# ConvFFN of a two-layer backbone: issue order of tiles 2 to 20 written out on four engines, partial sums grown in PSUM, all low parts of up weights on VectorE

## The chip, the cores and the metric

The kernel runs on one core of one Trainium2 chip. The metric is the device time of one execution in microseconds (us), the median of several runs. A profile is one execution taken by the hardware profiler. In it PE is the matrix engine (TensorE) and PEld its weight loads, DVE is VectorE, ACT is ScalarE, POOL is GpSimd, and SP is the queue that issues most DMAs. L306 means line 306 of the kernel's file.

## The reference

Two trunk layers run over 1024 latent tokens and (in the first layer only) 256 context tokens, all in float32, with 1024 channels. A layer is a mixer followed by a ConvFFN. This case is about the ConvFFN, which is the larger part of the time:

```python
def conv_ffn(h, w_up, conv_w, conv_b, w_down):
    L = h.shape[1]
    a = h @ w_up
    gate, val = a[..., :D_FF], a[..., D_FF:]
    gp = jnp.pad(gate, ((0, 0), (CONV_W // 2, CONV_W // 2), (0, 0)))
    g = gp[:, 0:L] * conv_w[0] + gp[:, 1:1 + L] * conv_w[1] + gp[:, 2:2 + L] * conv_w[2] + conv_b
    return (jax.nn.silu(g) * val) @ w_down
...
        x = x + g2 * conv_ffn(modulate(x, norm2_g[layer], sh2, sc2), ...)
```

D_FF is 2816. In the first layer (layer 0) latent and context tokens both pass through it, in the second (layer 1) only the latent tokens.

## The kernel before

**Precision.** Every float32 operand of a matmul is split into a high and a low part (`split`, L445 to L448): ACT writes the high part as a rounded copy (L447), then DVE or POOL writes the low part as source minus high part (L448). A product is three matmuls per chunk of 128 rows: high by high, high by low, low by high (`PASSES`).

**Halves and tiles.** The tokens of a layer are worked off in two halves: the positions of a half lie in two blocks of n columns (n is 320 and 324 in layer 0, 256 and 258 in layer 1). D_FF is cut into 22 tiles (f = 0 to 21) of 128 channels. So there are four halves of 22 tiles each, in order of time: two of layer 0, two of layer 1.

**The up projection of a tile** (`up`, L274) uses a seven-product scheme for a 2 by 2 block matrix product instead of eight. The weights of a tile form four blocks, A00 and A01 (gate), A10 and A11 (value); from these come the sums S1 = A10 + A11 (L241), S3 = A00 - A10 (L247), S2 = S1 - A00 (L248) and S4 = A01 - S2 (L251), all on POOL. Seven of these are weights of a product: A00 (P1), A01 (P2), S2 (P6), S1 (P5), S3 (P7), A11 (P4), S4 (P3). A product is 12 matmuls (4 chunks by 3 passes, L306), so a tile has 84. The moving operands (tile `hs`) are split once for each half in `operands`. The results are added to four blocks: c00 and c01 are the gate at the first and the last n positions, c10 and c11 the value. Every product has a PSUM bank of its own (tag `pq`, 8 banks in rotation); ACT copies P1 to c00 (L323), and seven DVE additions (L311) build the rest:

```python
add(c10, x["P6"], c00); add(c00, c00, x["P2"]); add(c01, x["P5"], c10)
add(c10, c10, x["P7"]); add(c11, c10, x["P5"]); add(c10, c10, x["P4"]); add(c01, c01, x["P3"])
```

**The gate.** ACT writes g = C0 * w1 + bias (L315, tile `g`, one buffer); DVE adds the two outer taps of the width-3 convolution (L317, L319; two pieces each in layer 0, where latent and context columns lie side by side, one each in layer 1); ACT applies Silu in place (L321); DVE multiplies with the value C1 (L361); the result is split into `act` (L362, so L447 on ACT and L448 on DVE).

**The down projection** (`down`, L368) runs beside it: in tile f it works on pairs of finished tiles, four output blocks D0 to D3 per tile (`downs`). Each is 12 matmuls of n columns (L376; in the first half of layer 1 it is 6 of 512 columns), and DVE adds it to the residual stream times a gain (L382). I call these additions X0 to X3. `prep` splits the down weights of a later tile (tile `wd`, two splits per tile) and issues the DMA of the next raw down weights (`fetch`, L261).

**Weights ahead.** During tile f the weights of tile f+1 are split, block by block, into slots that its products will read (tiles `wh` and `wq`, `steps`), and the raw blocks of tile f+2 are loaded: `load0` (A00, A01) and `load1` (A10, A11), 512 KB each (L236, tile `wr`, two buffers, so a load waits until the blocks that lie there are used up). When `load1` has landed, POOL makes S1 into the one buffer of tile `ws` (L241). While down projections run (`busy`), the low parts of A00, A01 and A11 are made by POOL (`POOL`, L245), those of the other four by DVE.

**Order.** The program is written tile by tile; a scheduler with its own model of time then sets the order on each engine, with `high_priority` for the additions, the gate and the `act` split. Engines run their instructions in the order so set, one after the other. Tiles 0 and 1 of a half hold no down projection; `beside` (`BESIDE`) adds small steps to tiles 1 to 3: in the first half of a layer the normalised input of the second half (L152, L153, with DMAs to a scratch in DRAM), in the second half of layer 0 sums of squares (L642, L644) and one square root (L658) for the next layer. Tile 21 holds no down projection either; the rest of them follows it.

## Time and profile before

| | us |
|---|---|
| median of 3 runs | 2914.65 (2911.54 to 2923.23) |
| the profiled execution's own time | 2920.99 |
| its span, first to last instruction | 2919.1 |

The mean granted clock of the profiled execution is 0.974 of full speed. Its time lies 6.3 us above the median of the runs, and 1.9 us of it lie outside the span. By the 88 groups of 84 up-projection matmuls the four halves stand at 486.8 to 926, 953.9 to 1378, 2107.9 to 2486 and 2512.3 to 2889 us of the span (from the first matmul of tile 0 to the end of tile 21's products); the mixers lie before and between the layers. "Stretch" below is a piece of the span; busy times in it are those of each engine, the number in brackets counts instructions.

### The profile page before, as it was taken

How to read it: one execution, taken by the hardware profiler on the slowest of the kernel's cores; microseconds unless marked ns; L12 is line 12 of the kernel's file. 1: busy time of each engine (PE TensorE's matmuls, PEld its weight loads, DVE VectorE, ACT ScalarE, POOL GpSimd, SP SyncE). 2: the span in 40 equal slices, each digit the busy share in tenths (PEclk: the TensorE clock that was granted, in tenths of full speed). 3: DMA queues.
4: the chain of work that ended last, by engine and by line, in shares of the span. 5: the costliest groups of instructions: out<-in, count | busy, mean ns of one | idle time of the engine just before them, and what ended most of it. 6: DMA issues, size and time to landing. Idle time of an engine off the chain costs nothing.

```text
span 2919.1 us, 47590 instructions
## 1 busy us (share of the span) xinstructions
PE 2772.8 (95%) x17978; PEld 2522.4 (86%) x17978; DVE 2216.9 (76%) x3748; ACT 1302.0 (45%) x2448; POOL 1267.9 (43%) x1044
## 2 busy tenths in 40 slices
...
GB/s 303 215 189 118 98 217 72 112 74 86 80 87 101 75 80 87 73 81 87 24 169 101 137 109 183 180 179 80 37 109 101 95 87 98 105 89 93 94 88 95
DMA packets 335886, 327.67 MB, mean 112 GB/s; under 512 B 16217, under 2 KB 264617, under 8 KB 335657
## 3 DMA queue, kind: packets, MB, share of 16 engines
...
q14 instruction: 86, 0.70, 0.1%
...
## 4 chain that ended last, share of the span: by engine, by line
PE 61%; DVE 14%; DMA 7%; POOL 7%; issue 5%; ACT 5%; SPq 0%; POOLq 0%; DVEq 0%; ACTq 0%
PE pq L306 18%; PE pq L478 15%; PE pq L376 11%; PE ps L478 6%; DMA wr<-in_ffn_w_up_dram 4%; POOL ws L241 2%; DVE xl L382 2%; DVE wh L448 2%; PE pq L566 2%; POOL wh L448 2%; DVE hx L311 2%; PE ps L487 2%; ACT t L1227 1%; POOL wr L248 1%; DMA wd<-in_ada_w_dram 1%
## 5 line engine op out<-in xcount | busy, mean ns | idle before, releaser
L376 PE MATMUL pq<-act,wd 128*128 128x320 f32 (+3 forms) x3696 | 639.8, 322 | 59.3 <-DVE xl L382 24.5
L376 PEld LDWEIGHTS pq<-act,wd 128*128 128x128 f32 x3696 | 557.1, 193 | 92.0 <-DVE xl L382 28.7
L306 PE MATMUL pq<-hs,wh 128*128 128x320 f32 (+3 forms) x4128 | 607.5, 299 | 16.3 <-DVE xl L382 7.8
L306 PEld LDWEIGHTS pq<-hs,wh 128*128 128x128 f32 x4128 | 576.9, 191 | 26.4 <-DVE xl L382 11.2
L306 PE MATMUL pq<-hs,wq 128*128 128x320 f32 (+3 forms) x3144 | 469.8, 299 | 8.4 <-DVE wq L448 4.9
L478 PE MATMUL pq<-hs,wh 128*128 128x512 f32 (+3 forms) x2100 | 469.0, 358 | 3.6 <-DVE hs L724 1.9
L306 PEld LDWEIGHTS pq<-hs,wq 128*128 128x128 f32 x3144 | 442.5, 191 | 14.1 <-DVE wq L448 5.7
L478 PEld LDWEIGHTS pq<-hs,wh 128*128 128x128 f32 x2100 | 365.8, 193 | 78.0 <-issue 6.2
L241 POOL TENSOR_TENSOR ws<-wr 128x512 f32<-128x512 f32 x88 | 153.6, 1745 | 397.3 <-DMA wr<-in_ffn_w_up_dram 333.0
L447 ACT ACTIVATE wh<-wr 128x512 fp32r<-128x512 f32 (+1 forms) x223 | 161.8, 726 | 354.0 <-POOL wr L248 201.5
L382 DVE SCALAR_TENSOR_TENSOR xl<-pq,mod,xl 128x320 f32<-128x320 f32 (+5 forms) x616 | 304.1, 514 | 11.7 <-PE pq L376 11.6
L448 DVE TENSOR_TENSOR wh<-wr,wh 128x512 fp32r<-128x512 f32 (+1 forms) x147 | 166.9, 1135 | 184.8 <-ACT wh L447 184.5
L448 POOL TENSOR_TENSOR wq<-wr,wq 128x512 fp32r<-128x512 f32 x152 | 235.7, 1550 | 32.9 <-ACT wq L447 32.9
L478 PE MATMUL ps<-hs,wh 128*128 128x512 f32 x840 | 240.0, 405 | 3.6 <-ACT hs L721 1.8
L311 DVE TENSOR_TENSOR hx<-hx,pq 128x320 f32<-128x320 f32 (+3 forms) x440 | 196.1, 448 | 29.1 <-PE pq L306 21.6
L447 ACT ACTIVATE wq<-wr 128x512 fp32r<-128x512 f32 x262 | 160.0, 623 | 101.3 <-PE pq L306 73.2
L447 ACT ACTIVATE wh<-ws 128x512 fp32r<-128x512 f32 x172 | 107.5, 625 | 169.8 <-PE pq L306 115.4
L478 PEld LDWEIGHTS ps<-hs,wh 128*128 128x128 f32 x840 | 141.9, 191 | 41.6 <-issue 14.4
L251 POOL TENSOR_TENSOR ws<-wr 128x512 f32<-128x512 f32 x88 | 120.2, 1366 | 123.3 <-DVE wh L448 112.3
L999 POOL TENSOR_TENSOR hsp<-hsq,hsp 128x512 fp32r<-128x512 f32 (+1 forms) x40 | 47.1, 1185 | 265.5 <-ACT hsq L998 265.5
L1006 DVE RECIPROCAL hsq<-hsq 128x512 f32<-128x512 f32 (+1 forms) x40 | 121.1, 3030 | 52.9 <-ACT hsq L1005 52.1
L448 DVE TENSOR_TENSOR wd<-wrd,wd 128x512 fp32r<-128x512 f32 x176 | 155.5, 912 | 0.2 <-ACT wd L447 0.2
...
## 6 DMA issues: line engine op xcount, KB each, us to landing
...
adaw<-in_ada_w_dram SPq DMA_DIRECT2D x128, 256.0 KB, 3.6
...
```

The lines of the kernel that those rows point to most:

```text
L241: op(raw["S1"], raw["A10"], raw["A11"], ALU.add)
L251: op(x, raw["A01"], raw["S2"], ALU.subtract)
L306: nc.tensor.matmul(o, w[wn][:, wp, k], self.part(s, bn, k, sp), start=(k == 0 and i == 0), stop=(k == 3 and i == 2))
L311: nc.vector.tensor_tensor(o, x, y, ALU.add)
L376: nc.tensor.matmul(pd, self.wds[j][i][:, wp, d % 4], self.acts[f][:, sp, lo:lo + m], start=(i == 0 and pi == 0), stop=(i == len(fs) - 1 an ...
L382: nc.vector.scalar_tensor_tensor(x, pd[:, a - lo:b - lo], net.mod[:, self.layer, st, 5, d:d + 1], x, ALU.mult, ALU.add)
L447: self.nc.scalar.activation(h, src, AF.Copy)
L448: return (e or self.nc.vector).tensor_tensor(l, src, f32(h), ALU.subtract)
L478: nc.tensor.matmul(o, w(wp, k), s(k, sp), start=(ki == 0 and pi == 0), stop=(ki == len(order) - 1 and pi == 2))
L487: nc.tensor.matmul(out, l[a], r[b], start=(first and i == 0), stop=(last and i == 2))
L566: nc.tensor.matmul(acc[32 * q:32 * q + 32, 0:256], self.sT[:, k, :], w[q // 2][:, 256 * (q % 2):256 * (q % 2) + 256], start=(k == 0), stop ...
L1006: nc.vector.reciprocal(r, r)
```

## The change

Four things change, all in `Ffn`, and all in tiles 2 to 20 of each half (those with `downs`).

1. **Order.** `run` opens a region at f = 2 and closes it at f = 21, in which PE, DVE, ACT and POOL issue in the order in which the program is written; SP's order is still the scheduler's. Inside it a tile is written as a list of tokens, `STEADY` (`STEADY2` for tile 2). A product is P1 to P7; D0 to D3 are the down blocks; X0 to X3 their additions to the residual; w with a name is a step of the weights (split, load or sum); c00, U, V and c10 are copies by ACT; c00+, c11+ and c01+ are additions by DVE; a token with a minus at its end belongs to the tile before. So Silu, the multiplication, the `act` split and X2 and X3 of a tile now stand among the first instructions of the next.
2. **Sums in PSUM.** P6 is accumulated onto P1's bank, P7 onto the same, and P4 onto the same (not in tile 2); P3 onto P5's bank. Between them ACT copies the bank out: P1 to c00, P1 + P6 to c01 (U), P1 + P6 + P7 to c10 (V), and with P4 to c10 again. DVE is left with c00 + P2, c11 = c10 + P5 and c01 + (P5 + P3). Matmuls are as many as before.
3. **Low parts.** `POOL` is empty: the low parts of A00, A01 and A11 are made by DVE. POOL keeps the four sums.
4. **Tile 1** leaves its Silu, multiplication and `act` split to tile 2.

```diff
-    POOL = ("A00", "A01", "A11")
+    POOL = ()
+    STEADY = ("P1", "silu-", "X2-", "X3-", "P2", "c00", "mul-", "wA00", "P6", "acth-", "c00+", "actl-", "wA01", "P5",
...
-        def product(p):
+        def product(p, onto=None):
             wn, bn = self.PROD[p]
-            o = net.t(net.ps, [P, 512], "pq" if p in ("P2", "P5") else "pq")[:, :n]
+            o = net.t(net.ps, [P, 512], "pq")[:, :n] if onto is None else onto
...
+                    nc.tensor.matmul(o, w[wn][:, wp, k], self.part(s, bn, k, sp),
+                                     start=(onto is None and k == 0 and i == 0), stop=(k == 3 and i == 2),
+                                     skip_group_check=onto is not None)
...
+            onto = dict(P6="P1", P7="P6", P3="P5")
+            if f > 2:
+                onto["P4"] = "P7"
+            ops = {"c00": lambda: copy(c00, x["P1"]), "c00+": lambda: add(c00, c00, x["P2"]),
+                   "U": lambda: copy(c01, x["P6"]), "V": lambda: copy(c10, x["P7"]),
+                   "c11+": lambda: add(c11, c10, x["P5"]), "c10": lambda: copy(c10, x["P4"]),
+                   "c10+": lambda: add(c10, c10, x["P4"]), "c01+": lambda: add(c01, c01, x["P3"]),
+                   "gate": gate, "taps": taps, "prep": prep}
...
+                if f == 2:
+                    region = self.net.tc.manual_schedule(engines={engines.PE, engines.DVE, engines.Activation, engines.Pool})
+                    region.__enter__()
+                if f == NF - 1:
+                    region.__exit__(None, None, None)
```

In `STEADY` the tile goes on: P5, U, P7, prep, D0, V, wS1, c11+, P4, wS2, X0, D1, c10, wS3, wload0, P3, wA11, wload1, X1, D2, c01+, gate, wS4, taps, D3, ws. On PE that is P1 P2 P6 P5 P7 D0 P4 D1 P3 D2 D3.

Three pieces show what this does to the order. The first is POOL in the second half of layer 1, one tile from its S1 on; before, it reads:

```order
L241 TENSOR_TENSOR ws_26590<-wr_26536 128x512
L247 TENSOR_TENSOR wr_26536<-wr_26500,wr_26536 128x512
L448 TENSOR_TENSOR wh_20746<-wr_26500,wh_20746 128x512
L448 TENSOR_TENSOR wq_20648<-wr_26500,wq_20648 128x512
L248 TENSOR_TENSOR wr_26500<-ws_26590,wr_26500 128x512
L251 TENSOR_TENSOR ws_26590<-wr_26500 128x512
L448 TENSOR_TENSOR wq_20973<-wr_26536,wq_20973 128x512
```

With the change the same engine there, up to the S1 of the next tile (lines are the changed file's):

```order
L248 TENSOR_TENSOR ws_26280<-wr_26242 128x512
L254 TENSOR_TENSOR wr_26242<-wr_26226,wr_26242 128x512
L255 TENSOR_TENSOR wr_26226<-ws_26280,wr_26226 128x512
L258 TENSOR_TENSOR ws_26280<-wr_26226 128x512
L248 TENSOR_TENSOR ws_26479<-wr_26441 128x512
```

The three low parts (`wh` and `wq`) are gone, and S2 (the third row now) no longer stands behind two of them.

The second piece is DVE at the turn of a tile in the same half: the last addition to c01, S4's low part (`wh` from `ws`), the taps (`g`), residual additions (`xl`), down weights (`wd`) and the multiplication (`g` from `hx`). Before:

```order
L311 TENSOR_TENSOR hx_26596<-hx_26596,pq_26742 128x258
L448 TENSOR_TENSOR wh_20747<-ws_26590,wh_20747 128x512
L382 SCALAR_TENSOR_TENSOR xl_3782<-pq_26760,mod_127,xl_3782 128x256
L382 SCALAR_TENSOR_TENSOR xl_3782<-pq_26768,mod_127,xl_3782 128x258
L317 SCALAR_TENSOR_TENSOR g_26597<-hx_26596,cols_175_786,g_26597 128x515
L382 SCALAR_TENSOR_TENSOR xl_3793<-pq_26776,mod_127,xl_3793 128x256
L382 SCALAR_TENSOR_TENSOR xl_3793<-pq_26784,mod_127,xl_3793 128x258
L319 SCALAR_TENSOR_TENSOR g_26597<-hx_26596,cols_175_786,g_26597 128x515
L448 TENSOR_TENSOR wd_26846<-wrd_26648,wd_26846 128x512
L448 TENSOR_TENSOR wd_26849<-wrd_26648,wd_26849 128x512
L361 TENSOR_TENSOR g_26597<-g_26597,hx_26596 128x516
```

With the change:

```order
L323 TENSOR_TENSOR hx_26282<-hx_26282,pq_26339 128x258
L524 TENSOR_TENSOR wh_20565<-ws_26280,wh_20565 128x512
L335 SCALAR_TENSOR_TENSOR g_26283<-hx_26282,cols_175_786,g_26283 128x515
L337 SCALAR_TENSOR_TENSOR g_26283<-hx_26282,cols_175_786,g_26283 128x515
L447 SCALAR_TENSOR_TENSOR xl_3782<-pq_26445,mod_127,xl_3782 128x256
L447 SCALAR_TENSOR_TENSOR xl_3782<-pq_26452,mod_127,xl_3782 128x258
L447 SCALAR_TENSOR_TENSOR xl_3793<-pq_26465,mod_127,xl_3793 128x256
L447 SCALAR_TENSOR_TENSOR xl_3793<-pq_26472,mod_127,xl_3793 128x258
L348 TENSOR_TENSOR g_26283<-g_26283,hx_26282 128x516
L524 TENSOR_TENSOR wh_20564<-wr_26425,wh_20564 128x512
L323 TENSOR_TENSOR hx_26481<-hx_26481,pq_26501 128x258
L346 TENSOR_TENSOR act_26532<-g_26283,act_26532 128x516
```

Both taps now stand ahead of X2 and X3, the down weights have moved to the middle of the next tile, and A00's low part (`wh` from `wr`) has come from POOL.

The third piece is DVE later in that tile of the changed program, from the low part of A01 on (two of the rows with `wq`, those of A01 and A11, were POOL's before, as the first piece shows; `wd` are the down weights, `wh` from `ws` S1, `wh` from `wr` S2, the second `wq` S3):

```order
L524 TENSOR_TENSOR wq_20466<-wr_26425,wq_20466 128x512
L524 TENSOR_TENSOR wd_26564<-wrd_26371,wd_26564 128x512
L524 TENSOR_TENSOR wd_26567<-wrd_26371,wd_26567 128x512
L524 TENSOR_TENSOR wh_20565<-ws_26479,wh_20565 128x512
L323 TENSOR_TENSOR hx_26481<-hx_26481,pq_26538 128x258
L524 TENSOR_TENSOR wh_20564<-wr_26425,wh_20564 128x512
L447 SCALAR_TENSOR_TENSOR xl_2932<-pq_26572,mod_127,xl_2932 128x256
L447 SCALAR_TENSOR_TENSOR xl_2932<-pq_26579,mod_127,xl_2932 128x258
L524 TENSOR_TENSOR wq_20467<-wr_26441,wq_20467 128x512
L524 TENSOR_TENSOR wq_20791<-wr_26441,wq_20791 128x512
```

A tile now has nine low parts on DVE, seven of up weights and two of down weights, where it had six, and three additions where it had seven. Outside the ConvFFN tiles PE, DVE, ACT and SP issue the same operations in the same sequence as before.

More of the change, by code (lines that the diff above doesn't have):

```diff
@@ L320, in gate, with high, low @@
                                                ALU.mult, ALU.add)
-            nc.scalar.activation(g, g, AF.Silu)
-        x = {}
-        todo = [("P1", lambda: nc.scalar.activation(c00, x["P1"], AF.Copy)),
+        def high():
+            self.acts[f] = self.act()
+            nc.scalar.activation(self.acts[f][:, 0, :2 * h.n], g, AF.Copy)
+        def low():
+            a = self.acts[f]
+            self.tail = nc.vector.tensor_tensor(a[:, 1, :2 * h.n], g, f32(a[:, 0, :2 * h.n]), ALU.subtract)
+        after = {"silu": lambda: nc.scalar.activation(g, g, AF.Silu),
+                 "mul": lambda: nc.vector.tensor_tensor(g, g, C1, ALU.mult), "acth": high, "actl": low}
+        x = {}
+        before, self.before = self.before, {}
+        if steady:
+            onto = dict(P6="P1", P7="P6", P3="P5")
[6 more added lines that the diff above has]
+                   "gate": gate, "taps": taps, "prep": prep}
+            i = 0
+            for tok in self.STEADY if f > 2 else self.STEADY2:
+                if tok in self.PROD:
+                    x[tok] = product(tok, x[onto[tok]] if tok in onto else None)
+                    if i in beside:
+                        beside[i]()
+                    i += 1
+                elif tok[0] == "D":
+                    adds["X" + tok[1]] = downs[int(tok[1])]()
+                elif tok[-1] == "-":
+                    if tok[:-1] in before:
+                        before[tok[:-1]]()
+                elif tok[0] == "X":
+                    adds.pop(tok)()
+                elif tok[0] == "w":
+                    if tok[1:] in steps:
+                        steps[tok[1:]]()
+                else:
+                    ops[tok]()
+            self.before = dict(after, **adds)
+            return
+        for fn in before.values():
+            fn()
+        todo = [("P1", lambda: copy(c00, x["P1"])),
                 ("P1 P6", lambda: add(c10, x["P6"], c00)),
@@ L358, in up @@
                     steps[st]()
-        act = self.acts[f] = self.act()
+        if f == 1:
+            self.before = after
+            return
         with net.tc.high_priority():
-            nc.vector.tensor_tensor(g, g, C1, ALU.mult)
-            self.tail = net.split(act[:, 0, :2 * h.n], act[:, 1, :2 * h.n], g)
+            for fn in after.values():
+                fn()
     def blocks(self, s):
```

51 lines of the change are left out of this document (32 added, 19 removed).

## The prediction

> **What bounds the kernel now.** I read the page first, then the busy times by stretch, the waits of the last half, its chain of waits, and at last the costs of single operations. The page's first part says that PE is the engine to look at:
>
> ```profile
> PE 2772.8 (95%) x17978; PEld 2522.4 (86%) x17978; DVE 2216.9 (76%) x3748; ACT 1302.0 (45%) x2448; POOL 1267.9 (43%) x1044
> ```
>
> 95% is a mean over stages, so I cut the span at the tiles. The columns are the stretch, its length, busy time and instructions of PE, PEld, DVE, ACT and POOL, granted clock, DMA share and GB/s. The first four rows are one tile of each half in which PE never waits, the next four tiles 5 to 20 of each half, the next four tiles 2 to 4, the last two single late tiles.
>
> ```profile
> core 0: us, PE busy (x) PEld busy (x) DVE busy (x) ACT busy (x) POOL busy (x), PEclk, DMA share, GB/s
> 700.66:720.08 19.42, 19.42 (x135) 19.42 (x133) 18.32 (x33) 7.99 (x14) 10.14 (x7) 1.00 0.28 82
> 1030.55:1050.09 19.54, 19.54 (x134) 19.54 (x133) 16.59 (x35) 9.05 (x15) 10.89 (x7) 1.00 0.27 81
> 2257.64:2273.15 15.51, 15.51 (x110) 14.46 (x108) 10.80 (x18) 7.30 (x13) 9.14 (x7) 1.00 0.31 93
> 2630.41:2646.30 15.89, 15.89 (x134) 15.89 (x133) 11.25 (x23) 6.66 (x12) 11.72 (x7) 1.00 0.23 66
> 601.70:914.10 312.40, 310.86 (x2115) 310.42 (x2114) 286.27 (x497) 128.24 (x209) 174.72 (x113) 1.00 0.27 82
> 1050.10:1366.10 316.00, 315.62 (x2114) 313.09 (x2113) 289.10 (x498) 128.87 (x209) 172.21 (x112) 1.00 0.27 81
> 2204.70:2476.00 271.30, 256.01 (x1729) 235.57 (x1728) 207.80 (x335) 116.36 (x208) 162.31 (x112) 0.98 0.32 94
> 2594.40:2878.80 284.40, 263.44 (x2114) 260.96 (x2113) 214.93 (x402) 117.88 (x210) 182.20 (x112) 0.98 0.30 89
> 530.80:601.70 70.90, 62.88 (x398) 59.70 (x396) 69.30 (x114) 32.51 (x57) 36.34 (x24) 0.98 0.37 108
> 981.40:1050.10 68.70, 63.47 (x414) 62.09 (x413) 63.46 (x104) 34.30 (x57) 44.61 (x30) 0.98 0.26 77
> 2145.20:2204.70 59.50, 51.59 (x327) 47.06 (x326) 55.27 (x77) 30.88 (x51) 38.98 (x25) 0.91 0.31 99
> 2539.50:2594.40 54.90, 49.34 (x397) 47.97 (x397) 50.21 (x84) 24.52 (x43) 36.62 (x24) 1.00 0.28 81
> ...
> 2646.30:2664.40 18.10, 16.15 (x135) 15.95 (x134) 13.29 (x27) 7.27 (x13) 11.25 (x7) 1.00 0.31 95
> 2681.60:2701.30 19.70, 17.65 (x134) 17.44 (x133) 14.90 (x30) 8.34 (x15) 11.51 (x7) 0.92 0.35 104
> ```
>
> A tile that PE alone sets takes 19.42, 19.54, 15.51 and 15.89 us in the four halves. Sixteen of these are 310.7, 312.6, 248.2 and 254.2 us, so tiles 5 to 20 stand above PE's own time by 1.7, 3.4, 23.1 and 30.2 us. Layer 0 is at its bound, with DVE busy for 92% (286.27 of 312.40); layer 1 is not. Three tiles of PE's time are 58.3, 58.6, 46.5 and 47.7, so tiles 2 to 4 stand above it by 12.6, 10.1, 13.0 and 7.2. In all some 101 us can be had, no more, since the matmuls stay as they are.
>
> Why layer 1 waits is in the waits of its second half (engine, tile and line, what it waited for: total us, times, longest):
>
> ```profile
> ACT wh L447 <- POOL wr L248: 77.6, 15, 5.3
> POOL ws L241 <- DMA wr<-in_ffn_w_up_dram: 77.3, 14, 5.9
> PE pq L376 <- DVE xl L382: 21.0, 12, 2.3
> ```
>
> and in the chain of waits there (start, length, what):
>
> ```profile
> 2662.74 5.15 DMA wr<-in_ffn_w_up_dram
> ...
> 2668.03 3.09 POOL ws L241
> ...
> 2672.79 1.74 POOL wh L448
> ...
> 2675.74 1.29 POOL wr L248
> 2677.05 0.64 ACT wh L447
> ...
> 2698.22 4.79 DMA wr<-in_ffn_w_up_dram
> ```
>
> It is a ring: a load lands, POOL makes S1, S3, two low parts, then S2; ACT, in order, copies S2 at 2677.05; DVE, in order, makes its low part, then the residual additions, whose PSUM banks PE waits for (21.0 us); and the low parts that end this free the buffer for the next load. Two rounds take 2698.22 - 2662.74 = 35.5 us, 17.7 each, which is the mean tile (284.40 / 16 = 17.8), not PE's 15.89.
>
> **The change part by part.** Prices from the last half, then from tiles 8 to 19 of the first half (mean ns of one behind the busy time):
>
> ```profile
> L247 POOL TENSOR_TENSOR wr<-wr,wr 128x512 f32<-128x512 f32 x16 | 26.1, 1631 | 1.2
> L447 ACT ACTIVATE wh<-ws 128x512 fp32r<-128x512 f32 x32 | 20.0, 625 | 12.0 <-POOL ws L241 6.2 <-PE pq L306 5.8
> L315 ACT ACTIVATE g<-hx,cols,cols 128x516 f32<-128x516 f32 x17 | 13.9, 820 | 52.1 <-DVE hx L311 52.1
> L317 DVE SCALAR_TENSOR_TENSOR g<-hx,cols,g 128x515 f32<-128x515 f32 x17 | 12.7, 747 | 0.0
> L321 ACT ACTIVATE g<-g 128x516 f32<-128x516 f32 x16 | 10.2, 637 | 11.4 <-DVE g L319 11.4
> ```
>
> ```profile
> L319 DVE SCALAR_TENSOR_TENSOR g<-hx,cols,g 128x511 f32<-128x511 f32 x13 | 17.9, 1374 | 0.0
> L448 DVE TENSOR_TENSOR wd<-wrd,wd 128x512 fp32r<-128x512 f32 x24 | 15.3, 678 | 0.0
> L448 DVE TENSOR_TENSOR wh<-wr,wh 128x512 fp32r<-128x512 f32 x12 | 14.9, 1244 | 0.2 <-ACT wh L447 0.2
> L315 ACT ACTIVATE g<-hx,cols,cols 128x640 f32<-128x640 f32 x13 | 12.0, 923 | 4.0 <-DVE hx L311 3.4 <-ACT wh L447 0.3
> L311 DVE TENSOR_TENSOR hx<-pq,hx 128x320 f32<-128x320 f32 x24 | 11.5, 481 | 0.0
> L317 DVE SCALAR_TENSOR_TENSOR g<-hx,cols,g 128x511 f32<-128x511 f32 x13 | 9.7, 746 | 0.1
> L319 DVE SCALAR_TENSOR_TENSOR g<-hx,cols,g 128x127 f32<-128x127 f32 x12 | 9.3, 771 | 0.0
> L321 ACT ACTIVATE g<-g 128x640 f32<-128x640 f32 x12 | 8.9, 740 | 24.5 <-DVE g L319 24.5
> L317 DVE SCALAR_TENSOR_TENSOR g<-hx,cols,g 128x127 f32<-128x127 f32 x13 | 7.6, 588 | 0.0
> L323 ACT ACTIVATE hx<-pq 128x320 f32<-128x320 f32 x12 | 5.0, 417 | 0.0
> ```
>
> One thing stands out: the same low part takes 0.68 us on DVE (`wd`) or 1.24 (`wh` from `wr`), the same tap 0.75 or 1.37. The first of each pair runs while POOL rests or nearly so, the second while it works; the additions that read PSUM are short throughout. I call these the cheap and the dear price.
>
> *The ring of layer 1.* With the low parts gone from POOL, S2 is ready 5.15 + 3.09 + 1.63 + 1.29 = 11.2 us after the load is issued. Then follow ACT's copy (0.63), the low parts of S2, S3 and A11, which free the buffer, and X0 among them (two pieces, at most c01's 0.48 each, 1.0). At the cheap price that is 11.2 + 0.6 + 3 x 0.68 + 1.0 = 14.8 us, at the dear one 16.5. I take the cheap price, because POOL's only operation near these three is now S4's sum; 14.8 is below PE's 15.51 and 15.89, so PE sets the tile. With 0.1 us left over per tile, 16 x 15.6 = 249.6 and 16 x 16.0 = 256.0: the gain is 21.7 and 28.4 us.
>
> In that the clock has a share: the tiles of 18.10 and 19.70 us differ little in their wait but in the granted clock, 1.00 and 0.92, and where PE doesn't wait it is 1.00. The Trainium skill, "TensorE: Matmul & The Clock Gate" (What's actually happening), has the clock halve after an idle window of about 3.4 us. By that no wait of 2.3 us would cost clock and this stretch would gain its idle time alone, 284.40 - 263.44 = 21.0 instead of 28.4 us; the trace disagrees, and I go by the trace.
>
> *DVE's load.* Four additions go (4 x 0.48 = 1.9 us a tile) and three low parts come (2.0 cheap, 3.7 dear). In layer 0 DVE works 286.27 / 16 = 17.9 us a tile; that becomes 18.0 to 19.7, against 19.42. I take the cheap end, since POOL has four operations a tile instead of seven; the cover is thin, and the dear end would cost 0.3 x 38 = 11 us in layer 0. In layer 1, 13.4 becomes 13.5 to 15.2, below PE. ACT gets three copies of 0.42 on 8 us a tile, hidden.
>
> *The new wait.* P6 now adds to P1's bank, so PE must wait until ACT has copied P1, and ACT's order puts Silu of the tile before ahead of that copy. From the end of P3 the path is c01+, gate, the copy and the low part of S4 (which DVE does ahead of the taps), taps, Silu, copy. Queued behind it on PE are P5, P7 and all else, and on ACT U and V. In layer 0: 0.48 + 0.92 + 0.63 + 0.68 + (2 x 0.75 + 0.59 + 0.77) + 0.74 + 0.42 = 6.7 us, and six handovers between engines, for which I put 0.3 us (POOL's to ACT in the chain above took 0.02 us, from 2675.74 + 1.29 to 2677.05; the DMA's to POOL 0.14): 7.0. PE has D2, D3, P1 and P2 to do meanwhile, 48 of a tile's 132 matmuls: 19.42 x 48 / 132 = 7.06. In layer 1: 0.48 + 0.82 + 0.63 + 0.68 + 2 x 0.75 + 0.64 + 0.42 + 0.3 = 5.5 against 15.89 x 48 / 132 = 5.78. So it is hidden, barely. S1's sum on POOL can reach the taps only if the load lands early; it is issued near the end of P3 and takes 5 us, so I take the cheap price. At the dear one for S4's low part and the taps of full width, P6 would wait 8.8 - 7.06 = 1.7 us in layer 0 and 7.3 - 5.78 = 1.5 in layer 1.
>
> *Tiles 5 to 20 of layer 0.* Nothing much to gain: at 19.45 and 19.6 a tile, 1.2 and 2.4 us.
>
> *Tiles 2 to 4.* In the first half DVE is busy for 69.30 of 70.90 us. The steps of `beside` stay; each writes one buffer that a DMA must have read, and DVE now waits for it in order, and ACT's copy of P1 behind it. Between none of the excess and all of it removed I take half to six tenths in the first half and in those of layer 1 (8, 6.5 and 4.4 us). In layer 0's second half the square root comes, in ACT's order, ahead of the copy of P1 in tile 3, with two small additions before it: some five operations of 0.4 to 0.6 us, 3 us, so I take 2.7 of 10.1. Sum 21.6, bounds 43 (all) and -10 (each of the ten wide steps in tile 2 makes PE wait 1 us).
>
> *Sum.* 21.7 + 28.4 + 1.2 + 2.4 + 21.6 = 75.3 us. The profiled execution's own time of 2920.99 becomes 2845.7; it stands 6.3 us above the median, so 2914.65 - 75.3 = 2839.4, say 2840.
>
> **The rivals.**
>
> A, *P6 waits for the copy of P1* (slower). If POOL's S1 falls into the taps, tiles 2 to 20 of each half pay 1.7 us in layer 0 and 1.5 in layer 1: 38 x 1.7 + 38 x 1.5 = 122 us, 2840 + 122 = 2962. It decides from about 75 / 76 = 1.0 us a tile on. For it: 7.0 of 7.06 us; the dear taps of layer 0 are in the trace. Against it: S1 has to wait for a landing of about 5 us and for S4's low part, which stands ahead of the taps. The Trainium skill, "SBUF — State Buffer" (Who interferes with whom), makes this an exclusive lock: a DVE instruction with two SBUF inputs and a POOL instruction that reads SBUF exclude each other for a whole instruction, PSUM readers aside. The pairs 0.68 and 1.24, 0.75 and 1.37 agree.
>
> B, *the ring still sets layer 1*, at the dear 16.5 us: 32 x 16.5 = 528 of 271.3 + 284.4, a gain of 27.7 instead of 50.1. That gives 2862. For it: S1 took 3.09 us on POOL because DVE was at work, and DVE does more now. So the change would not do what it says there.
>
> **How the numbers follow.** Forecast 0.70, B 0.14, A 0.16, and of A 0.08 at its full price, 0.06 near two thirds of it (about 2921, no change), 0.02 below. About 0.5%, 14.6 us, is what a measurement of this kernel can tell: faster 0.86, same 0.06, slower 0.08. The low end of the range is all excess removed, 2914.65 - 101 = 2814; the high end takes in B, starts that gain nothing and the dear DVE load: 2862 + 21.6 + 11 = 2895. What is left out is A.
>
> **What would show it.** Right: tiles 5 to 20 at about 311, 314, 250 and 256 us by stretch, clock 1.00 there; four POOL operations a tile; no wait of ACT for S2's sum. Wrong: a wait of PE for ACT's copy of P1 in every tile (A); tiles of 16.5 us in layer 1 with PE waiting at P7 or at D2 (B); DVE busy for the whole of a layer 0 tile (its dear load); tiles 2 to 4 longer than now.

## The result and the profile after

The changed kernel takes 2966.09 us (2959.72 to 2970.28, 4 runs); the kernel before, on the same chip, 2914.90 (2911.54 to 2923.23, 4 runs). The ratio is 1.0169, with a 95% interval of 1.0141 to 1.0198. The change makes it slower by 1.7%, where 2840 us and a gain were forecast. The profiled execution takes 2966.70 us.

The page's first part for the changed kernel:

```profile
PE 2769.4 (93%) x17978; PEld 2515.7 (85%) x17978; DVE 2301.2 (78%) x3676; ACT 1354.3 (46%) x2672; POOL 872.7 (29%) x816
```

PE is busy for 2769 us as it was for 2773 before: the matmuls cost the same, and what came on top is waiting. POOL has lost a third of its work. Where the waiting lies is in the busy times by stretch (columns as in the prediction; first tiles 2 to 4 of the four halves, then tiles 5 to 20):

```profile
532.50:614.40 81.90, 63.98 (x398) 63.08 (x397) 66.06 (x111) 34.94 (x66) 21.28 (x16) 0.87 0.31 94
1009.67:1091.60 81.93, 66.95 (x414) 66.05 (x413) 65.02 (x99) 36.69 (x64) 30.64 (x21) 0.88 0.24 71
2195.24:2264.77 69.53, 51.42 (x326) 46.82 (x325) 58.74 (x80) 33.41 (x62) 23.09 (x16) 0.88 0.32 102
2594.32:2656.22 61.90, 50.26 (x398) 49.19 (x397) 56.62 (x84) 29.12 (x56) 23.21 (x16) 0.92 0.31 91
614.40:943.12 328.72, 314.19 (x2115) 310.02 (x2114) 294.45 (x484) 137.94 (x257) 92.94 (x65) 1.00 0.26 78
1091.60:1422.62 331.02, 317.21 (x2114) 312.95 (x2113) 295.71 (x484) 138.50 (x257) 90.56 (x64) 1.00 0.26 77
2264.77:2532.80 268.03, 253.20 (x1729) 232.40 (x1728) 245.51 (x321) 129.12 (x257) 88.05 (x64) 1.00 0.31 95
2656.22:2924.61 268.39, 260.11 (x2114) 255.34 (x2113) 246.70 (x387) 128.88 (x256) 88.60 (x64) 1.00 0.31 92
```

Against the rows of before, tiles 2 to 4 are longer by 11.0, 13.2, 10.0 and 7.0 us (41.2 in sum), tiles 5 to 20 by 16.3 and 15.0 in layer 0, and shorter by 3.3 and 16.0 in layer 1. Together that is +53.3 us; the span grew by 45.7 (2964.8 against 2919.1), so the rest of the program became some 7.6 us shorter; what made that stays open.

In PE's waits (what it waited for: total us, times, longest) the changed kernel has one entry that stands alone:

```profile
PE pq L317 <- ACT hx L326: 111.1, 74, 11.6
```

These are up products that wait for ACT's copies out of a bank (`hx` from `pq`, L326), the wait that the change adds. One tile of layer 0 shows how it comes about. The timeline has start, length, what, and in brackets how long the engine was idle before and what ended that (its first line is the load of A10 and A11, which S1 waits for):

```profile
794.37 0.37 SPq L243 DMA_DIRECT2D wr<-in_ffn_w_up_dram  x1
...
795.28 3.69 PE L437 MATMUL pq<-act,wd 128*128 128x320 f32 x24
795.48 0.49 DVE L323 TENSOR_TENSOR hx<-hx,pq 128x320 f32<-128x320 f32 x1
796.00 0.92 ACT L329 ACTIVATE g<-hx,cols,cols 128x640 f32<-128x640 f32 x1 [2.53 <-DVE hx L323]
...
797.47 0.69 DVE L524 TENSOR_TENSOR wh<-ws,wh 128x512 fp32r<-128x512 f32 x1 [1.51 <-ACT wh L523]
798.08 0.74 DVE L335 SCALAR_TENSOR_TENSOR g<-hx,cols,g 128x511 f32<-128x511 f32 x1
798.30 1.68 POOL L248 TENSOR_TENSOR ws<-wr 128x512 f32<-128x512 f32 x1 [6.74 <-DVE wh L524]
...
798.86 1.67 DVE L337 SCALAR_TENSOR_TENSOR g<-hx,cols,g 128x511 f32<-128x511 f32 x1
800.06 1.62 POOL L254 TENSOR_TENSOR wr<-wr,wr 128x512 f32<-128x512 f32 x1
...
800.45 1.37 DVE L335 SCALAR_TENSOR_TENSOR g<-hx,cols,g 128x127 f32<-128x127 f32 x1
...
802.31 0.74 ACT L347 ACTIVATE g<-g 128x640 f32<-128x640 f32 x1 [4.87 <-DVE g L337]
...
802.95 0.42 ACT L326 ACTIVATE hx<-pq 128x320 f32<-128x320 f32 x1
...
803.42 1.29 PE L317 MATMUL pq<-hs,wh 128*128 128x320 f32 x7 [0.94 <-ACT hx L326]
```

P3 ends at 795.28 and the copy of P1 at 803.37: 8.1 us, where the forecast had 7.0. The order is as forecast, S4's low part and then the taps. But S1's sum on POOL (L248) starts at 798.30, here as soon as S4's low part has left the `ws` buffer (in 11 of 17 cases in this half it was the load's landing), and S3's (L254) right behind it. The second tap, beside S1, takes 1.67 us and the third, 127 columns wide, takes 1.37 beside S3; the last one, beside none, takes 0.35 in the part left out. P6 waits 0.94 us.

Tile 2 of each half is a second place. In the last half, timeline of the changed kernel:

```profile
2603.97 0.82 ACT L329 ACTIVATE g<-hx,cols,cols 128x516 f32<-128x516 f32 x1
...
2605.40 0.74 DVE L335 SCALAR_TENSOR_TENSOR g<-hx,cols,g 128x515 f32<-128x515 f32 x1
...
2607.02 0.63 ACT L347 ACTIVATE g<-g 128x516 f32<-128x516 f32 x1 [2.23 <-DVE g L337]
2607.56 0.37 ACT L326 ACTIVATE hx<-pq 128x258 f32<-128x258 f32 x1
...
2607.99 1.23 PE L317 MATMUL pq<-hs,wh 128*128 128x258 f32 x4 [9.43 <-ACT hx L326]
```

The gate, taps and Silu here are those of tile 1, whose work on DVE lags; P6 of tile 2 waits 9.43 us for the copy that ACT does behind that Silu. The granted clock of tiles 2 to 4 is 0.87 to 0.92, where it was 0.91 to 1.00. The Trainium skill, "TensorE: Matmul & The Clock Gate" (What's actually happening), expects just that behind a wait longer than its idle window of about 3.4 us; here the trace agrees.

### The profile page after: what moved, and what is told of

Read it like the earlier page. It is cut to its first block, busy times and chain, and to the rows that moved or that the text cites. A ratio compares the mean times of both kernels' runs of the same rounds, so it can differ in the third digit from the quotient of the medians.

```text
span 2964.8 us, 46865 instructions
## 1 busy us (share of the span) xinstructions
PE 2769.4 (93%) x17978; PEld 2515.7 (85%) x17978; DVE 2301.2 (78%) x3676; ACT 1354.3 (46%) x2672; POOL 872.7 (29%) x816
## 4 chain that ended last, share of the span: by engine, by line
PE 58%; DVE 26%; issue 5%; ACT 5%; DMA 4%; POOL 1%; SPq 0%; ACTq 0%; DVEq 0%; POOLq 0%
PE pq L317 16%; PE pq L554 14%; PE pq L437 8%; PE ps L554 6%; DVE wh L524 5%; DVE g L337 4%; DVE g L335 3%; DVE xl L447 3%; DVE wq L524 2%; DVE hx L323 2%; ACT wh L523 2%; PE pq L642 2%; PE ps L563 2%; DVE hs L524 1%; DVE wd L524 1%
## 5 line engine op out<-in xcount | busy, mean ns | idle before, releaser
L317 PE MATMUL pq<-hs,wh 128*128 128x320 f32 (+3 forms) x4128 | 624.9, 304 | 109.9 <-ACT hx L326 104.7
L437 PE MATMUL pq<-act,wd 128*128 128x320 f32 (+3 forms) x3696 | 609.1, 316 | 8.3 <-DVE xc L447 3.6
L524 DVE TENSOR_TENSOR wh<-wr,wh 128x512 fp32r<-128x512 f32 (+1 forms) x223 | 290.1, 1301 | 69.3 <-ACT wh L523 67.0
L248 POOL TENSOR_TENSOR ws<-wr 128x512 f32<-128x512 f32 x88 | 125.0, 1420 | 609.5 <-DMA wr<-in_ffn_w_up_dram 479.7
L326 ACT ACTIVATE hx<-pq 128x320 f32<-128x320 f32 (+3 forms) x312 | 125.8, 403 | 222.4 <-PE pq L317 188.9
L524 DVE TENSOR_TENSOR wh<-ws,wh 128x512 fp32r<-128x512 f32 x172 | 121.8, 708 | 131.9 <-ACT wh L523 131.7
L524 DVE TENSOR_TENSOR wq<-wr,wq 128x512 fp32r<-128x512 f32 x262 | 191.4, 752 | 16.6 <-ACT wq L523 16.6
L258 POOL TENSOR_TENSOR ws<-wr 128x512 f32<-128x512 f32 x88 | 117.1, 1330 | 285.4 <-DVE wh L524 269.5
L347 ACT ACTIVATE g<-g 128x640 f32<-128x640 f32 (+3 forms) x88 | 60.4, 686 | 285.6 <-DVE g L337 285.6
L255 POOL TENSOR_TENSOR wr<-ws,wr 128x512 f32<-128x512 f32 x88 | 122.2, 1388 | 179.2 <-DVE wh L524 172.3
L329 ACT ACTIVATE g<-hx,cols,cols 128x640 f32<-128x640 f32 (+3 forms) x88 | 76.7, 872 | 214.6 <-DVE hx L323 213.2
## 6 DMA issues: line engine op xcount, KB each, us to landing
adaw<-in_ada_w_dram SPq DMA_DIRECT2D x128, 256.0 KB, 3.4
```

What stands on the lines that cost most here:

```text
L248: op(raw["S1"], raw["A10"], raw["A11"], ALU.add)
L255: op(x, raw["S1"], x, ALU.subtract)
L258: op(x, raw["A01"], raw["S2"], ALU.subtract)
L317: nc.tensor.matmul(o, w[wn][:, wp, k], self.part(s, bn, k, sp), start=(onto is None and k == 0 and i == 0), stop=(k == 3 and i == 2), skip ...
L326: nc.scalar.activation(o, x, AF.Copy)
L437: nc.tensor.matmul(pd, self.wds[j][i][:, wp, d % 4], self.acts[f][:, sp, lo:lo + m], start=(i == 0 and pi == 0), stop=(i == len(fs) - 1 an ...
```

## The experiments

Two theories stood at first. **Copy**: PE is held up because P6 grows on P1's bank and must let ACT copy P1 first, behind Silu and the taps. **Load**: with nine low parts DVE is full, and the waits only show that. A name such as "tiles 5 to 20: a, b, c, d" gives the four halves in order of time, in us; line numbers are those of each kernel's own file. Times of before, measured beside each group, were 2914.82 us (first four kernels run), 2918.87 (next four), 2915.05 (next four) and 2916.54 (last one). Tiles 2 to 4 are given as the sum over the four halves: 254.0 before, 295.3 after.

### Layer 0: what makes P6 wait

**Taps first.** In both lists the taps move ahead of S4's split:

```diff
-  ... "c01+", "gate", "wS4", "taps", "D3", "ws")
+  ... "c01+", "gate", "taps", "wS4", "D3", "ws")
```

> The changed kernel, with the taps of a tile issued ahead of S4's split (copy and low part) instead of behind it. Theory C (the copy of P1): PE waits at P6 because ACT's copy of P1 stands behind Silu, Silu behind the taps, and POOL's S1 and S3 fall into the taps. S1 cannot start before S4's low part has left its buffer, so with the taps first POOL is out of them and the path from P3 to P6 gets some 3 us shorter: layer 0 tiles fall from 20.6 to 19.4 to 19.7 us, layer 1 tiles from 16.8 to 15.6 to 16.3, the long waits in tile 2 stay; total 2900 to 2925 us. Theory L (load): nine low parts a tile have made DVE the bound, the wait at P6 is only where PE meets it; order does not change DVE's work, so layer 0 tiles stay at 20.4 or more and the total at 2955 to 2970.

Measured: 2910.05 us, ratio 0.9987 (0.9974 to 1.0001). Tiles 5 to 20: 310.1, 312.9, 265.9, 269.0; tiles 2 to 4: 278.5. One exchange in each list gives back 56 us (2966.09 - 2910.05). Layer 0 stands at PE's own time with nine low parts a tile. But the exchange also made DVE's own work shorter, from 294.45 to 274.71 us in the first half, which the theory of the load had ruled out, so this run alone doesn't separate the two. Layer 1 hardly moves, which the theory of the copy did not expect.

**Copy first.** ACT's copy of P1 moves ahead of Silu:

```diff
-    STEADY = ("P1", "silu-", "X2-", "X3-", "P2", "c00", "mul-", ...
+    STEADY = ("P1", "c00", "silu-", "X2-", "X3-", "P2", "mul-", ...
-    STEADY2 = ("P1", "silu-", "P2", "c00", "mul-", ...
+    STEADY2 = ("P1", "c00", "silu-", "P2", "mul-", ...
```

> The changed kernel, with ACT's copy of P1 issued ahead of Silu of the tile before. Theory C: P6 no longer hangs on the taps; the waits at P6 go, in layer 0 tiles of 19.4 to 19.8 us, in tile 2 the wait shrinks from 8 to 12 us by the Silu and the multiplication's part only (2 to 4 us); a new wait may show at P7, for the copy of P1 + P6, which stands behind the high part of act. Total 2900 to 2930 us. Theory L: layer 0 stays at 20.4 or more, total 2955 to 2970.

Measured: 2950.53 us, ratio 1.0124 (1.0100 to 1.0149). Tiles 5 to 20: 325.4, 326.7, 266.4, 268.2. Both numbers of the copy's theory are missed: taking the copy of P1 out from behind Silu gives 3 to 4 us a half in layer 0 (the load's total, 2955 to 2970 us, is missed as well). The timeline of one tile of this kernel shows why (first the copy of P1, now early, then the chain behind the taps):

```profile
801.54 0.44 ACT L326 ACTIVATE hx<-pq 128x320 f32<-128x320 f32 x1 [3.32 <-PE pq L317]
...
803.09 0.74 ACT L347 ACTIVATE g<-g 128x640 f32<-128x640 f32 x1 [1.11 <-DVE g L337]
...
805.83 0.74 ACT L342 ACTIVATE act<-g 128x640 fp32r<-128x640 f32 x1 [1.49 <-DVE g L348]
...
807.00 0.42 ACT L326 ACTIVATE hx<-pq 128x320 f32<-128x320 f32 x1
...
807.47 2.04 PE L317 MATMUL pq<-hs,wq 128*128 128x320 f32 x12 [0.67 <-ACT hx L326]
```

P6 no longer waits, but P7 does, for the next copy (U), which stands behind `act`'s high part, the multiplication, Silu and the late taps. The wait has moved by one product.

**No bank reads.** The first two copies read elsewhere, so that P6 and P7 need nothing of ACT; the kernel leaves out what they carry, P1 in c00 and P1 + P6 in c01:

```diff
+            away = f32(self.part(s, "B00", 0, 0))
-            ops = {"c00": lambda: copy(c00, x["P1"]), ... "U": lambda: copy(c01, x["P6"]),
+            ops = {"c00": lambda: copy(c00, away), ... "U": lambda: copy(c01, away),
```

> The changed kernel, in which ScalarE's first two copies of a written-out tile (P1's bank to c00, P6's bank to c01) read an operand slab in place of the bank, so that P6 and P7 grow on banks that nobody reads in between; it leaves out what these copies carry (P1 in c00, the sum in c01). The work of every engine is the same. If P6 and P7 are held up only by those copies in ScalarE's order (copy), tiles 5 to 20 of layer 0 fall from 329 and 331 us to 310 to 316, tiles 2 to 4 lose 10 to 35 of their 295 us, and the time is 2895 to 2925 us. If VectorE's load sets the tile (load), the waiting reappears elsewhere and it stays at 2945 us or above.

Measured: 2931.66 us, ratio 1.0057 (1.0041 to 1.0073). Tiles 5 to 20: 316.3, 317.8, 267.1, 270.3; tiles 2 to 4: 279.3. PE's waits in this kernel:

```profile
PE pq L438 <- DVE act L346: 31.3, 31, 2.3
...
PE pq L317 <- ACT hx L326: 7.0, 4, 5.3
```

Most of the gain comes, but less than the copy's theory wanted: 2932 for 2895 to 2925. The waiting for copies is gone (7.0 us for 111.1), and more than a quarter of it returns one station on, the larger part in layer 1: the down matmuls wait for `act`'s low part, which also stands behind the taps. In layer 0's first half, 6 us above PE's own time, DVE works for 292.13 us and waits 24.5 us for ACT's copies of weights, which together fill the 316.32 us.

**Own banks.** The written order with a bank for every product, as before; three copies of ACT go and DVE gets four additions more, so that it makes the seven of before again (one more than the expectation counts):

```diff
-            onto = dict(P6="P1", P7="P6", P3="P5")
-            if f > 2:
-                onto["P4"] = "P7"
+            onto = {}
...
+                   "U": lambda: add(c10, x["P6"], c00), "W": lambda: add(c01, x["P5"], c10),
+                   "V": lambda: add(c10, x["P7"], c10), ... "c10": lambda: add(c10, c10, x["P4"]),
```

> The changed kernel in its written-out order, but each product in a bank of its own as before: P6, P7, P4 and P3 don't grow on another product, and three copies of ScalarE become three adds of VectorE (0.45 us each in the kernel before, so 1.3 us a tile). If growing on P1's bank is what makes P6 wait (copy), its waiting for ScalarE's copy goes below 15 us in all and tiles 5 to 20 of layer 0 fall to 312 to 325 us each; if VectorE bounds layer 1 (load there), its tiles rise by 0.8 to 1.4 us each, to 280 to 292 us a half, and the time is 2935 to 2985 us. If the order itself, and not the banks, is the cause in layer 0, that stays at 328 us or more; if VectorE does not bound layer 1, that stays at 268 us, and the time with layer 0 freed is 2915 to 2935 us.

Measured: 3010.18 us, ratio 1.0326 (1.0311 to 1.0341). Tiles 5 to 20: 337.0, 336.7, 277.8, 285.9. PE's waits:

```profile
PE pq L436 <- DVE act L346: 61.0, 38, 2.6
```

No wait for a copy is left, as the copy's theory said, and yet layer 0 is slower still, which it excluded; the second case, that the order itself is the cause in layer 0 (328 us or more), is what came. Layer 1 rises by 0.6 and 1.1 us a tile, about as expected of a full DVE, and the total lies above every range. So the loss doesn't need sums that grow in PSUM: without them DVE works for longer (311.16 us in layer 0's first half for 294.45, and 23.6 us of waiting for ACT's copies of weights, which nearly fills the 336.95), and the down matmuls wait for the low part that ends its chain. What growing alone costs, this run can't tell, since it also gives DVE four additions more. The copy is the place where the late taps first reach PE. What is left to tell apart is why the taps are late: S4's split ahead of them, or POOL's sums beside them; "taps first" removed both.

**S1 held.** The order of the changed kernel stays, but POOL, ahead of S1, copies one column of the gate, which the last tap writes:

```diff
         def taps():
...
+            if steady:
+                nc.gpsimd.tensor_copy(self.t([P, 1], "hold", bufs=1), g[:, c + m - 2:c + m - 1])
```

> The changed kernel with its order as it is (S4's split ahead of the taps), and on GpSimd, ahead of S1's sum, a copy of one column of the gate that waits for the last tap; so S1 and S3 can't run beside the taps, and nothing else moves. It adds that copy, which Silu then waits for. If S1 and S3 on the taps are what the forecast's path from P3 to the copy of P1 missed (collision), the taps take 0.75 and 0.35 us again, P6's waiting falls under 0.3 us a tile in layer 0, its tiles 5 to 20 take 310 to 318 us in each half and the time is 2905 to 2940 us. If S4's split ahead of the taps is enough by itself to make P6 wait (split), layer 0 stays at 323 us or more a half and the time at 2945 us or above.

Measured: 2919.98 us, ratio 1.0008 (0.9992 to 1.0023). Tiles 5 to 20: 310.1, 312.9, 268.1, 268.7; tiles 2 to 4: 281.7. A tile of layer 0 in its timeline:

```profile
784.75 0.69 DVE L526 TENSOR_TENSOR wh<-ws,wh 128x512 fp32r<-128x512 f32 x1 [1.51 <-ACT wh L525]
...
785.36 0.75 DVE L335 SCALAR_TENSOR_TENSOR g<-hx,cols,g 128x511 f32<-128x511 f32 x1
...
786.14 0.75 DVE L337 SCALAR_TENSOR_TENSOR g<-hx,cols,g 128x511 f32<-128x511 f32 x1
786.81 0.35 DVE L335 SCALAR_TENSOR_TENSOR g<-hx,cols,g 128x127 f32<-128x127 f32 x1
787.19 0.35 DVE L337 SCALAR_TENSOR_TENSOR g<-hx,cols,g 128x127 f32<-128x127 f32 x1
...
787.68 0.18 POOL L340 COPY hold<-g 128x1 f32<-128x1 f32 x1 [8.12 <-DVE g L337]
...
787.82 1.29 POOL L248 TENSOR_TENSOR ws<-wr 128x512 f32<-128x512 f32 x1
...
787.89 0.74 ACT L349 ACTIVATE g<-g 128x640 f32<-128x640 f32 x1 [3.17 <-POOL hold L340]
...
788.54 0.42 ACT L326 ACTIVATE hx<-pq 128x320 f32<-128x320 f32 x1
```

S4's split stands ahead of the taps as in the changed kernel, and an operation and a wait more stand on the path; still layer 0 is at PE's own 310.1 and 312.9 us. The four taps take 2.2 us and the copy of P1 is over at 788.96, 0.6 us before P6 starts at 789.59. DVE's work in layer 0's first half falls from 294.45 to 276.97 us. So S1 and S3 on the taps are the cause of layer 0's loss, and S4's split by itself is not. Layer 1, whose taps S1 didn't meet (0.75 us each in the changed kernel), stays where it was.

### Tiles 2 to 4: where the written part begins

**From tile 3.** Tile 2 is scheduled as before with its own banks, tile 1 ends itself, and the written part begins at tile 3:

```diff
-        steady = len(downs) > 0
+        steady = f > 2 and len(downs) > 0
...
+            for fn in downs[:dict(P4=1, P3=3).get(p, 0)]:
+                fn()()
+            downs = downs[dict(P4=1, P3=3).get(p, 0):]
...
-        if f == 1:
+        if f == 2:
             self.before = after
...
-                if f == 2:
+                if f == 3:
                     region = ...
```

> The changed kernel, with the written-out part begun at tile 3: tile 2 of each half is scheduled and has a bank for each product as before (its low parts all on DVE), and tile 1 ends itself. Theory C: the waits of 8 to 12 us at P6 of tile 2 come from the copy of P1 behind the end of tile 1, whose DVE work lags; with separate banks PE runs on, and tiles 2 to 4 fall from 295 us in the four halves together to 255 to 270; the later tiles stay at 20.6 and 16.8; total 2925 to 2945 us. If tiles 2 to 4 are long because DVE's load in them is (theory L), the wait moves to tile 3 and the total stays within 10 us of 2966.

Measured: 2945.09 us, ratio 1.0115 (1.0095 to 1.0136); tiles 2 to 4: 265.6, tiles 5 to 20 as in the changed kernel (328.7, 332.3, 266.0, 269.2). Of the 41 us that the starts lost, 30 come back; the rest of the program is some 7 us longer in the profiled execution, so the whole gains 21.0. The edit takes three things from tile 2 at once, the written order, the shared banks and tile 1's unfinished work; that the last of them is the cause rests on the timeline above, not on this run.

**Both.** Taps first, and from tile 3 (the two edits above together).

> Two repairs of the changed kernel together: the taps stand ahead of S4's split, and the written-out part begins at tile 3. If the waiting for the copy of P1 has these two causes and no third (copy), tiles 5 to 20 are as with the taps first (310, 313, 266, 269 us) and tiles 2 to 4 as with the start at tile 3 (265 us in sum) or a few us below: 2880 to 2900 us. If VectorE's load is behind both (load), the two repairs overlap and the time stays at 2905 us or above.

Measured: 2887.00 us (2884.63 to 2894.74), ratio 0.9890 (0.9868 to 0.9913): it beats both kernels. Tiles 5 to 20: 310.1, 312.9, 266.1, 269.8; tiles 2 to 4: 259.7. The two repairs add up (56.0 and 21.0 us alone, 79.1 together), so they mend two things, though not wholly apart: in tiles 2 to 4 they give 16.8 and 29.7 us alone and 35.6 together. In its rows for tiles 5 to 20 layer 0 has no wait left (PE busy for the whole stretch); layer 1 has:

```profile
607.87:917.95 310.08, 310.08 (x2114) 310.08 (x2113) 274.69 (x482) 139.81 (x257) 83.40 (x64) 1.00 0.27 82
...
2200.83:2466.97 266.14, 255.78 (x1729) 233.13 (x1728) 251.92 (x320) 128.92 (x256) 90.50 (x64) 1.00 0.31 95
2582.58:2852.38 269.80, 261.79 (x2115) 255.80 (x2114) 255.78 (x386) 129.57 (x258) 88.76 (x64) 1.00 0.31 92
```

**Both, and copy first** (three edits together).

> Both repairs, and ScalarE's copy of P1 ahead of the Silu as well. If with both repairs P6's waiting for that copy is the last thing that the order of ScalarE costs (copy), it falls below 0.3 us a tile and the time goes 5 to 20 us below that of both repairs alone. If what is left is VectorE's (load, or sums that stop it), the waiting only moves from P6 to P7 and the time is the same within 8 us.

Measured: 2895.07 us, ratio 0.9915 (0.9895 to 0.9934); tiles 5 to 20: 310.1, 312.8, 266.2, 269.3; tiles 2 to 4: 261.3. No gain: the median lies 8.1 us above that of both repairs, the profiled execution at the same time (2894.69 and 2894.74 us), about as the second case said; the order of ACT is not what holds layer 1.

**From tile 4.** Both repairs, and the start one tile later (`f > 3`, and 3 and 4 in the two other places).

> The kernel with both repairs, and the written-out part begins at tile 4 in place of 3. If the start costs what tile 1 leaves undone and no more (copy), tiles 2 to 4 go from 259.8 us in sum to about those of the scheduled kernel with nine low parts on VectorE, 250 to 256, and tiles 5 to 20 stay at 310, 313, 266 and 269: 2878 to 2888 us. If the written order has to find its pace anew wherever it begins (lag), tile 4 takes over tile 3's excess and the time is 2885 to 2900 us.

Measured: 2892.41 us, ratio 0.9919 (0.9893 to 0.9945); tiles 2 to 4: 262.0. Tile 4 takes 21.0, 21.1, 22.8 and 20.1 us instead of 20.2, 19.5, 17.1 and 16.4: wherever the written order begins, its first tile is longer. Why it is, these runs don't show.

### Layer 1: ring or load

**Lows on POOL.** The changed kernel, with the low parts of A00, A01 and A11 back on POOL:

```diff
-    POOL = ()
+    POOL = ("A00", "A01", "A11")
```

> The changed kernel, with the low parts of A00, A01 and A11 on POOL again. Theory L: DVE is rid of three low parts, 2 to 3.7 us a tile, so layer 0 tiles fall to 19.4 to 19.8 us and the total to 2935 or less. Theory C: POOL has seven operations a tile again, the taps are met as often or more, and the ring through POOL is back in layer 1: layer 0 tiles 20.4 to 21.5, layer 1 tiles 17 to 18.5, total 2966 to 3020 us.

Measured: 2970.94 us, ratio 1.0205 (1.0185 to 1.0225). Tiles 5 to 20: 325.1, 327.2, 274.6, 282.2; tiles 2 to 4: 287.5. Layer 0 hardly profits from a DVE with three instructions fewer, and layer 1 loses 6.6 and 13.8 us. As in the forecast, it is the low parts' leaving POOL that brings layer 1's gain.

**Lows only.** The kernel before with one line of the change and nothing else:

```diff
-    POOL = ("A00", "A01", "A11")
+    POOL = ()
```

> One part of the change alone: the kernel before, in its scheduled order and with its own banks, but all nine low parts of weights on VectorE. If the three low parts on GpSimd are what kept layer 1 above its product time (the ring), tiles 5 to 20 of layer 1 fall from 271.3 and 284.4 us to about 266 to 270 each and layer 0 stays near 312 to 318: 2890 to 2915 us. If nine low parts make VectorE the bound (load), layer 0 goes to 320 us or more in each half and layer 1 gains nothing: 2920 to 2950 us.

Measured: 2896.46 us, ratio 0.9921 (0.9900 to 0.9943). Its rows for tiles 5 to 20:

```profile
596.37:906.80 310.43, 310.43 (x2115) 310.43 (x2113) 283.35 (x545) 127.92 (x209) 104.26 (x65) 1.00 0.28 82
...
2190.03:2457.88 267.85, 255.47 (x1737) 234.89 (x1736) 242.14 (x387) 116.53 (x208) 111.25 (x64) 0.99 0.32 95
2576.74:2853.29 276.55, 265.02 (x2115) 256.61 (x2114) 239.95 (x447) 116.76 (x208) 126.08 (x64) 1.00 0.30 89
```

One line of the change alone makes the kernel faster by 0.8%, and layer 0 bears nine low parts without a wait, with seven additions as before. The written order and the sums in PSUM, in the form of the changed kernel, cost some 70 us on top of it; with both repairs they gain some 9 in the median (2884.63 to 2894.74 us against 2895.93 to 2899.43). In the profiled executions tiles 5 to 20 are shorter by 9.1 us, of it 6.8 in the last half, and tiles 2 to 4 longer by 6.1.

**Sums on DVE.** Both repairs, and in the tiles concerned the four sums of weights on DVE:

```diff
-        op = nc.gpsimd.tensor_tensor
+        def op(*a):
+            (nc.vector if self.busy else nc.gpsimd).tensor_tensor(*a)
```

> The kernel with both repairs, and in tiles 2 to 20 the four sums of weights on VectorE in place of GpSimd. If VectorE loses about as much to each GpSimd sum that runs beside it (1.67 in place of 0.68 us for a low part) as such a sum would cost on VectorE itself (port), tiles 5 to 20 of layer 1 fall from 266 to 269 us to 255 to 265 and layer 0 stays at 310 to 316: 2865 to 2895 us. If VectorE is simply full (load), four more instructions of 0.68 us a tile come on top: layer 1 at 290 to 310 us, layer 0 at 325 or more, 2930 to 3000 us.

Measured: 2889.60 us, ratio 0.9894 (0.9876 to 0.9912). Tiles 5 to 20: 310.1, 312.9, 263.0, 269.5. The time is that of both repairs, in the port's range; of layer 1's halves the first reaches 255 to 265 us and the second doesn't. DVE is no longer full there, 231.17 us busy of 262.96, because now DVE itself waits for the loads; DVE's waits in tiles 5 to 20 of that half:

```profile
DVE ws L238 <- DMA wr<-in_ffn_w_up_dram: 16.4, 16, 1.3
```

So four instructions more on DVE cost nothing, which the theory of the load excluded: what POOL's sums took from DVE by running beside it was more, since with the sums added DVE's work fell from 251.92 to 231.17 us.

**Two lows out.** Both repairs; in tiles 2 to 20 of layer 1 the kernel leaves out the low parts of A01 and A11, and the products take old ones:

```diff
             x = raw[name]
+            if self.layer == 1 and self.busy and name in ("A01", "A11"):
+                nc.scalar.activation(slots[name][:, 0], x, AF.Copy)
+                return
```

> The kernel with both repairs; in tiles 3 to 20 of layer 1 it leaves out the low parts of A01 and A11, two of VectorE's nine (the products take old ones). If VectorE is the bound of layer 1 (load), which stands at 16.63 and 16.86 us a tile against 15.51 and 15.89 of its products, the two give back 1.4 to 2.5 us a tile as far as the products allow: tiles 5 to 20 fall to 248 to 258 us in both halves, 2850 to 2872 us in all. If something else holds layer 1 (the ring of loads and sums, ScalarE's order), they stay at 264 to 270 and the time at 2880 to 2892 us.

Measured: 2855.23 us, ratio 0.9792 (0.9775 to 0.9809). Tiles 5 to 20 of layer 1:

```profile
2188.56:2437.53 248.97, 248.97 (x1730) 231.62 (x1729) 234.23 (x289) 132.67 (x257) 93.86 (x64) 1.00 0.33 102
2553.24:2807.48 254.24, 254.24 (x2114) 254.24 (x2113) 236.90 (x354) 132.97 (x257) 92.22 (x64) 1.00 0.32 96
```

17.7 and 18.9 us of DVE's work are gone, and the stretches are shorter by 17.2 and 15.6, down to PE's own 248 and 254. These low parts also stand in the ring that frees the buffers for the next load, so the run alone would leave the ring as a rival. DVE's waits in the kernel with both repairs, tiles 5 to 20 of layer 1's first half, settle it; this is the only one:

```profile
DVE g L335 <- ACT g L329: 14.2, 16, 0.9
```

DVE works for 251.92 us and waits 14.2 us for ACT's gate, which fills the 266.14; it waits neither for a load nor for POOL. With that, layer 1's bound in the repaired kernel is DVE, work and this wait together.

## Why the prediction was wrong, step by step

**What bounds the kernel.** Right: PE's own time for tiles 5 to 20 (310.7, 312.6, 248.2 and 254.2 us) came out within 0.8 us in "two lows out", which reaches it in all four halves.

**The ring of layer 1.** Right in its cause, too large in size. "Lows on POOL" and "lows only" show that the ring was broken by that edit. But the gain was 3.3 and 16.0 us, not 21.7 and 28.4. The cheap price was taken for the low parts "because POOL's only operation near these three is now S4's sum". S2's low part met just that sum, and others met other sums. Groups of DVE in tiles 5 to 20 of layer 1's first half, changed kernel (mean ns of one behind the busy time):

```profile
L524 DVE TENSOR_TENSOR wh<-wr,wh 128x512 fp32r<-128x512 f32 x32 | 56.2, 1758 | 0.0
...
L524 DVE TENSOR_TENSOR wq<-wr,wq 128x512 fp32r<-128x512 f32 x48 | 31.3, 678 | 0.0
L346 DVE TENSOR_TENSOR act<-g,act 128x512 fp32r<-128x512 f32 x16 | 27.7, 1732 | 0.0
```

The low parts of A00 and S2 (`wh` from `wr`) and that of `act` stand beside POOL's sums and pay over 1 us each on the 0.68 of the others (`wq`).

**The clock's share.** Right: the granted clock there is 1.00, for 0.98 before.

**DVE's load.** This step failed in layer 1. The 18.4 us a tile in layer 0 (294.45 / 16) lie within 18.0 to 19.7. In layer 1 "13.5 to 15.2, below PE" became 245.51 / 16 = 15.3, and with both repairs 15.7 and 16.0, against PE's 15.51 and 15.89. And the step has no term for what DVE, in order, waits for. DVE's waits in tiles 5 to 20 of the changed kernel, the first line layer 0's first half, the other layer 1's (beside the first one stand 0.7 us of waiting for PE):

```profile
DVE wh L524 <- ACT wh L523: 30.9, 31, 1.5
...
DVE wh L524 <- ACT wh L523: 22.5, 16, 1.4
```

These are ACT's copies of S4 and, in layer 0, of S1 (`wh`), which stand behind the gate and behind V. In layer 1 work and waits are 245.51 + 22.5 = 268.0 us, the whole of the 268.03: DVE sets the tile there, as it does with both repairs, and the ring doesn't, since DVE waits for no load and no sum. In layer 0 they are 294.45 + 30.9 + 0.7 = 326.1 of 328.72: there too DVE had next to nothing to spare, but only with the dear taps; with S1 held its work is 17.5 us less, and PE sets the tile. So nine low parts alone don't bound layer 0 (S1 held, lows only), and the two theories meet there: what made the copy late also made DVE full. Rival B had the size right (16.5 us a tile forecast, 268.03 / 16 = 16.75 measured), with the ring as its cause.

**The new wait.** This step failed in layer 0. The order, the place and the sum of undisturbed durations were right: with S1 held the copy of P1 comes 0.6 us ahead of P6. What failed is the sentence that S1's sum "can reach the taps only if the load lands early", with the cheap price for the taps. The load was issued as forecast, "near the end of P3": at 794.37 in the tile shown, 0.9 us ahead of it. It had landed by 798.16, when S4's low part ended, so it took at most 3.8 us, not 5. But by its own numbers the forecast was too bold: with 5 us from the end of P3 on S1 starts at 5.0, and the taps run from 0.48 + 0.92 + 0.63 + 0.68 = 2.7 to 5.6 us. S4's low part, which POOL had to wait for, protected nothing, since the taps come right behind it. The mis-sized term is the four taps: 2.9 us in the sum, 4.1 in the tile shown (0.74 + 1.67 + 1.37 + 0.35). The bound of the dear price, 8.8 us, and the measured 8.1 are near; of the two ends I took the wrong one. In sum the excess of layer 0 over the forecast is 17.5 and 17.4 us.

**Tiles 2 to 4.** This step failed most: a gain of 21.6 us was forecast, with -10 as the far bound, and 41.2 were lost. I priced what DVE had to do there, but not that ACT's order puts the copy of P1 behind the Silu of tile 1, which lags at that point; P6's wait there is 9.43 us in the half shown, and the clock falls as well. "From tile 3" gives 30 of the 41 us back, "S1 held" 13.6, most of it in tiles 3 and 4 of layer 0.

**The sum.** The forecast for the profiled execution was 2845.7 us. To it come 17.5 + 17.4 in layer 0, 18.4 + 12.4 in layer 1 (268.03 - 249.6 and 268.39 - 256.0) and 62.9 in tiles 2 to 4, less 7.6 in the rest: 121.0, which is the measured 2966.7.

**The rivals.** A (2962 us) named the mechanism of layer 0, POOL's S1 on the taps, and the Trainium skill's rule in "SBUF — State Buffer" (Who interferes with whom) spoke for it: an exclusive lock for a whole instruction, so that a short one pays as much as a long one. The tap of 127 columns agrees, 0.35 us alone and 1.37 beside a sum of 1.62. A's price was 1.7 us a tile against 1.2 measured (328.72 - 310.1 = 18.6 us over 16 tiles), and its 1.5 in layer 1 was DVE's load instead: PE waits for the copy there too, but the taps keep their 0.75 us. That its total is so near is in part chance: half of the loss against the forecast lies in tiles 2 to 4, where A had only its price per tile.
